# Building C with the gate in ScalarE's operand of the one-hot product while the top-k runs, one comparison on VectorE, and five paces set anew

## The chip, the cores and the metric

The kernel runs on one core of one Trainium2 chip. The metric is the device time of one execution in microseconds (us): three runs of the kernel before took 3491.34, 3493.19 and 3498.84 us, median 3493.19. Engines are named as in the profile: PE is TensorE, DVE is VectorE, ACT is ScalarE, POOL is GpSimd, SP is SyncE.

## The reference, cut to what matters

One encoder layer over 1024 tokens of width 1024: two attention branches, a merge, a layer norm, and then a layer of product-key experts. Only the last part is touched. Each token has 8 heads, each head picks 16 experts out of 128 x 128 by two top-16 searches over 128 keys and one over their sums:

```
s = jnp.einsum('thpd,hpkd->thpk', q, sub_keys)
top_s, top_i = lax.top_k(s, K)
cand_i = top_i[:, :, 0, :, None] * PEER_N_KEYS + top_i[:, :, 1, None, :]
...
gate = jax.nn.softmax(best_s, axis=-1)
h = jax.nn.gelu(jnp.einsum('thkd,td->thk', u_table[idx], xb))
return jnp.einsum('thk,thkd->td', gate * h, v_table[idx])
```

So each token has 128 selections: a key i, a key j and a gate. All of it is float32.

## The kernel before

The 1024 tokens are eight tiles of 128. Five of them (0, 1, 2, 6, 7) are **gathered**: for each of a token's 128 selections one row of `u` and one row of `v` (4 KB each) is fetched by an indirect DMA that POOL issues, 128 rows (512 KB) at a time. Three of them (3, 4, 5, `DENSE`) are **dense**: their hidden states are multiplied with all 16384 experts, and a table C of 128 x 128 gates per token says which count.

The end of the kernel, from `dense_block` on, is what matters here. It has two stages.

**Building C** (lines 1579 to 1627). Selection c of a token puts its gate at place (i, j). For one token this is a product of two one-hot matrices, A (128 selections x 128 keys i) and B (128 selections x 128 keys j), one of which carries the gate. `onehot(t4)` makes A (`a`) and B (`b`) for four tokens, 384 tokens in all, so 96 blocks. PE makes four matmuls of a block (tile `v`, "`v<-ab`"), and ACT copies the result out of PSUM in two parts, 44 columns into `C` (line 1623) and 84 into `S` (line 1624); each eight blocks SP writes `S` to DRAM (`cd`). Step k of the loop makes the operands of block k + 3 (`BLEAD`), the matmuls of block k, and the copies of block k - 1. The tile `ab` has four buffers, so the operands of block k + 4 wait for the matmuls of block k; `v` has three.

In `onehot`, `b` is made by DVE in four instructions, each a comparison with the key's number and a multiplication by the gate (line 1570). `a` is made by DVE in one comparison of 512 columns (line 1576) for even blocks. For odd blocks ACT makes it as Relu(1 - |n - i|): four Abs with the key's number as bias (line 1573) and one Relu of 512 columns (line 1574).

**The dense loop** (128 steps) multiplies hidden states with `u` (tile `b`, 24 matmuls a step) and the gated result with `v` (18 matmuls), and streams both tables, 1 MB a step, through SP's queue (`uraw<-ut`, `vraw<-vt`). ACT and DVE split the float32 data into two parts.

Two queues of other work are fed into both stages. `mm` calls `tick` for each matmul, which adds the matmul's nominal time times a rate to a credit, and steps are taken from the queue while the credit lasts. So the rates, not the time, set what stands beside what in the order of each engine.

- **V** (rate `RATEV`, first number in building C, second in the dense loop) handles the gathered tiles' `v` rows: a pair of gathers (line 1852, tile `vr`, or places lent by C), a copy of the gates into `win` by ACT (line 1879), and four matmuls (tile `pg`). 256 pairs in all. `win` has four slots, so a copy waits for the matmuls four pairs back.
- **B** (rate `RATEB`, first number in building C, second in the dense loop, third there once the last top-k is done) handles the top-k of tiles 4, 5 and 6 (`LATE`, tags k4, k5, k6), then the `u` rows of tile 6 (line 1469, and the dot product on DVE, line 1481) mixed with the top-k of tile 7, then tile 7's `u` and `v` rows. A dense tile's top-k must be complete before its blocks begin: `selections` forces it (k4 at block 32, k5 at block 64) and loads gate, i and j into `cT`.

PE's, DVE's and POOL's orders in this part are the order of the code. ACT's and SP's are set by the scheduler that builds the program.

Of the kernel before, what the change touches and what calls it, by code (L numbers as in the profile page):

```python
# [10 lines left out]
F32 = mybir.dt.float32  # L11
# [4 lines left out]
AF = mybir.ActivationFunctionType  # L16
OP = mybir.AluOpType
# [10 lines left out]
TKI = 1  # L28
RATEP = (0.975, 0.975, 0.87)

RATEB = (2.1, 0.562, 0.58)
RATEV = (4.2, 0.425)
SEL = (1, 2, 3)
DENSE = (3, 4, 5)
GATHERED = (0, 1, 2, 6)
# [1 line left out]
LATE = (4, 5, 6)  # L37
# [4 lines left out]
HALF, LOOP, GROUP, BLK = 44, 8, 4, 32  # L42
VCOST = 3.0
XAT = 14
AENG = "XY"
UPOOL = (0, 0)
VPAT = ()
VBUF = 3
# [226 lines left out]
def mm(g, o, l, r, start, stop_):  # L275
    g.pe.matmul(o, l, r, start=start, stop=stop_)  # L276
    n = 1
    for d in r.shape[1:]:
        n *= d
    us = max(n, 256) / 2400.0 if r.dtype == F32R else max(4 * n, 256) / 2400.0  # L280
    g.V.tick(us)
    if not g.V.busy:
        g.B.tick(us)
# [98 lines left out]
def run(gen):  # L382
    for _ in gen:
        pass
# [19 lines left out]
def body(ctx, g):  # L404
# [106 lines left out]
    g.pp = ctx.enter_context(tc.tile_pool(name="pp", bufs=1))  # L511
    C = g.pp.tile([128, len(DENSE), HALF, 128], F32, name="C")
    dense_block(g, C)


# [998 lines left out]
def dense_block(g, C):  # L1514
# [3 lines left out]
    dve, act, pool, sp, pe = g.dve, g.act, g.pool, g.sp, g.pe  # L1518
    tiles = DENSE
    nt = len(tiles)  # L1520
    n = nt * 128
# [13 lines left out]
    def hidden_states():  # L1535

        for i, t in enumerate(tiles):
            z = bp.tile([128, 2, 4, 128], F32, name="ab").rearrange("p a b c -> p (a b c)")
            sp.dma_start(z, g.x1d[t])
            for k in range(0, 8, 4):  # L1540
                yield
                pt = g.psV.tile([128, 4, 128], F32, name="v21")
                for u in range(4):
                    pe.transpose(pt[:, u, :], z[:, (k + u) * 128:(k + u + 1) * 128], ident)
                s = slice(i * 128, (i + 1) * 128)
                split(g, xh[:, k:k + 4, s], xl[:, k:k + 4, s], pt)

    def selections(i):

        if i == 0:  # L1550
            yield
            yield
        g.B.need(f"k{tiles[i]}")
        cij = bp.tile([128, 3, 128], F32, name="cij", bufs=1)
        sp.dma_start(cij, g.cijd[tiles[i]])
        yield
        pt = g.psV.tile([128, 4, 128], F32, name=f"v{i}1")
        for j in range(3):
            pe.transpose(pt[:, j, :], cij[:, j, :], ident)
        act.copy(cT[:, :, i * 128 - 128:i * 128], pt[:, 0:3, :])  # L1560
        yield

    def onehot(t4):

        cT_, t4_ = (g.rows.cT, t4) if t4 < 32 else (cT, t4 - 32)
        ab_ = bp.tile([128, 2, 4, 128], F32, name="ab")
        a, b = ab_[:, 0], ab_[:, 1]
        for u in range(4):
            t = slice(4 * t4_ + u, 4 * t4_ + u + 1)
            dve.tensor_scalar(b[:, u, :], g.iota, cT_[:, 2, t], cT_[:, 0, t], op0=OP.is_equal, op1=OP.mult)  # L1570
        if AENG[t4 % len(AENG)] == "Y":
            for u in range(4):
                act.activation(a[:, u, :], g.iota, AF.Abs, scale=-1.0, bias=cT_[:, 1, 4 * t4_ + u:4 * t4_ + u + 1])
            act.activation(a, a, AF.Relu, scale=-1.0, bias=1.0)
        else:
            dve.tensor_tensor(a, g.iota[:, None, :].to_broadcast([128, 4, 128]), cT_[:, 1, 4 * t4_:4 * t4_ + 4, None].to_broadcast([128, 4, 128]), op=OP.is_equal)
        return a, b

    g.B.rate, g.V.rate = RATEB[0], RATEV[0]
    zx = ExitStack()  # L1580
# [7 lines left out]
    with tc.tile_pool(name="bp", bufs=BLEAD + 1) as bp, tc.tile_pool(name="cj", bufs=2) as cj:  # L1588
        ab, pb = {}, {}
        cT = bp.tile([128, 3, n - 128], F32, name="cT", bufs=1)  # L1590
        for k in range(-BLEAD - 4, n4 + 1):
            e = k + BLEAD + 4
            if e % 32 in (0, 4) and e < n4:
                if e % 32 == 0:
                    sel = selections(e // 32)
                next(sel)
            if 0 <= k + BLEAD < n4:
                ab[k + BLEAD] = onehot(k + BLEAD)
            if k > 0 and (k + 8) % 32 == 0 and (k + 8) // 32 in later:
                g.rows.places.drop(later[(k + 8) // 32] + lent.get((k + 8) // 32, []))  # L1600
            if k > 0 and k % 32 == 0 and k // 32 in later:
                g.rows.leave(later[k // 32] + lent.get(k // 32, []))
                for p in lent.pop(k // 32, []):
                    g.keys.give(p)
            if 0 <= k < n4:
                a, b = ab.pop(k)
                pb[k] = g.psV.tile([128, 4, 128], F32, name=f"v{k % 3}0")
                for u in range(4):
                    mm(g, pb[k][:, u, :], a[:, u, :], b[:, u, :], True, True)
            if k == n4 - XAT:  # L1610
                xp = zx.enter_context(tc.tile_pool(name="xp", bufs=1, side="right"))
                xh = xp.tile([128, 8, n], F32R, name="xh")
                xl = xp.tile([128, 8, n], F32R, name="xl")
                xt = hidden_states()
            if xt and k % 2 == 0:
                next(xt, None)
            if k > 0:
                e = k - 1
                i, o = 4 * e // BLK, 4 * e % BLK
                if o == 0:  # L1620
                    S = cj.tile([128, 128 - HALF, BLK], F32, name="S")
                p = pb.pop(e).rearrange("p t j -> p j t")
                act.copy(C[:, e // 32, :, 4 * e % 128:4 * e % 128 + 4], p[:, 0:HALF, :])
                act.copy(S[:, :, o:o + 4], p[:, HALF:128, :])  # L1624
                if o + 4 == BLK:
                    sp.dma_start(g.cd[i], S)
        run(xt)
    g.B.rate, g.V.rate = RATEB[1], RATEV[1]
    u_hl, v_hl, c_hl, phs = {}, {}, {}, {}
# [99 lines left out]
    for j in range(128):  # L1729
# [14 lines left out]
        if f"k{LAST}" in g.B.done:  # L1744
            g.B.rate = RATEB[2]
        if j == 126:
# [3 lines left out]
        k = (j + 1 - LOOP) // 8 * nt  # L1750
# [279 lines left out]
```

## Time and profile before

| | |
|---|---|
| median of three runs | 3493.19 us |
| the profiled execution's own time | 3488.81 us |
| its span, first to last instruction | 3487.0 us |
| building C, first to last copy into `S` | 1763.7 to 2177.9 us |
| dense loop, first to last `h` | 2200.1 to 3450.9 us |
| DMA, mean over the span | 325 GB/s |
| granted TensorE clock, mean | 0.932 |

Instructions of one engine can overlap at their edges, so the duration of one is more than what it adds to a row of them; "busy" in a group or a window counts overlapped time once.

### The profile page before, as it was taken

How to read it: one execution, taken by the hardware profiler on the slowest of the kernel's cores; microseconds unless marked ns; L12 is line 12 of the kernel's file. 1: busy time of each engine (PE TensorE's matmuls, PEld its weight loads, DVE VectorE, ACT ScalarE, POOL GpSimd, SP SyncE). 2: the span in 40 equal slices, each digit the busy share in tenths (PEclk: the TensorE clock that was granted, in tenths of full speed). 3: DMA queues.
4: the chain of work that ended last, by engine and by line, in shares of the span. 5: the costliest groups of instructions: out<-in, count | busy, mean ns of one | idle time of the engine just before them, and what ended most of it. 6: DMA issues, size and time to landing. Idle time of an engine off the chain costs nothing.

```text
span 3487.0 us, 54632 instructions
## 1 busy us (share of the span) xinstructions
PE 3089.3 (89%) x20141; PEld 2301.4 (66%) x20141; DVE 2376.6 (68%) x5489; ACT 1140.0 (33%) x2380; POOL 1756.1 (50%) x1430
## 2 busy tenths in 40 slices
PE   7899898999998878789777777999999999999996
PEld 5577776885566666567633332688887777777875
DVE  3234523358988898987479865687777767677776
ACT  3443223232432222111134443334333333333332
POOL 2032115325565456553464567555756566566761
PEclk9999999998998887989988989999999999999998
DMA  8373347889989778989998899999999999999995
GB/s 282 118 250 113 98 151 264 296 320 324 306 301 368 255 271 309 352 323 373 369 377 340 340 371 392 376 371 372 409 409 406 400 401 391 402 400 397 399 398 196
DMA packets 366876, 1132.22 MB, mean 325 GB/s; under 512 B 49456, under 2 KB 85936, under 8 KB 364816
## 3 DMA queue, kind: packets, MB, share of 16 engines
q0 software_dynamic: 184448, 671.56, 50.8%
q1 hardware_dynamic: 165760, 428.06, 33.7%
q10 hardware_dynamic: 16400, 29.11, 2.2%
q8 instruction: 158, 2.59, 0.3%
q14 instruction: 110, 0.90, 0.1%
HBM read 995.94 MB, written 132.64 MB: 324 GB/s over the span
## 4 chain that ended last, share of the span: by engine, by line
PE 47%; DVE 19%; DMA 16%; issue 7%; POOL 3%; ACT 2%; another core or an unknown queue 0%; SPq 0%; ACTq 0%; POOLq 0%; DVEq 0%
PE b L276 12%; PE v L276 10%; DMA uraw<-ut 8%; PE pj L276 7%; PE s L276 5%; PE o L276 5%; DVE g L1481 4%; PE pg L276 3%; DMA g<-u,idx 3%; PE S L276 2%; DVE ab L1570 1%; POOL g L1469 1%; DMA vr<-v,ve 1%; PE a L276 1%; DMA wl<-whd 1%
## 5 line engine op out<-in xcount | busy, mean ns | idle before, releaser
L1469 POOL DMA_INDIRECT g<-u,idx x569 | 685.3, 1204 | 609.0 <-DVE hh L1481 311.8
L1481 DVE CUSTOM_DVE_ANT_0 g<-g,ext 128x1024 f32<-128x1024 f32 x569 | 701.1, 1238 | 85.2 <-DMA g<-u,idx 66.8
L1852 POOL DMA_INDIRECT vr<-v,ve x285 | 338.1, 1186 | 174.0 <-PE pg L276 74.5
L276 PE MATMUL b<-xh,uh 128*128 128x384 f32 x1024 | 354.3, 346 | 41.0 <-ACT h L1684 39.7
L294 POOL TENSOR_TENSOR wl<-wraw,wh 128x1024 fp32r<-128x1024 f32 x63 | 152.7, 2424 | 436.7 <-ACT wh L293 337.2
L276 PE MATMUL b<-xl,uh 128*128 128x384 f32 x1024 | 352.1, 344 | 0.0
L276 PE MATMUL b<-xh,ul 128*128 128x384 f32 x1024 | 351.7, 343 | 0.1
L294 DVE TENSOR_TENSOR ul<-uraw,uh 128x512 fp32r<-128x512 f32 x256 | 176.0, 690 | 223.1 <-ACT uh L293 205.0
L276 PE MATMUL v<-vl,ch 128*128 128x512 f32 x768 | 301.9, 393 | 0.7 <-DVE vl L294 0.6
L276 PE MATMUL v<-vh,ch 128*128 128x512 f32 x768 | 301.1, 392 | 0.1
L276 PE MATMUL v<-vh,cl 128*128 128x512 f32 x768 | 300.9, 392 | 0.0
L276 PE MATMUL pj<-xh,wh 128*128 128x512 f32 x624 | 283.7, 455 | 13.9 <-ACT xh L293 7.1
L293 ACT CAST uh<-uraw 128x512 fp32r<-128x512 f32 x256 | 157.2, 620 | 410.2 <-PE b L276 210.0
L276 PE MATMUL pg<-vr,win 128*32 128x512 f32 x1364 | 243.2, 641 | 46.8 <-DMA vr<-v,ve 38.7
L276 PE MATMUL pj<-xl,wh 128*128 128x512 f32 x624 | 257.8, 413 | 2.4 <-DVE xl L294 2.4
L276 PE MATMUL pj<-xh,wl 128*128 128x512 f32 x624 | 257.5, 413 | 0.0
L276 PEld LDWEIGHTS b<-xh,uh 128*128 128x128 f32 x1024 | 196.3, 192 | 62.2 <-ACT h L1684 48.1
L276 PEld LDWEIGHTS v<-ab 128*128 128x128 f32 x768 | 111.1, 214 | 187.8 <-issue 113.4
L293 ACT CAST vh<-vraw 128x512 fp32r<-128x512 f32 x256 | 156.1, 618 | 162.1 <-PE v L276 115.5
L276 PEld LDWEIGHTS b<-xl,uh 128*128 128x128 f32 x1024 | 196.1, 192 | 15.2 <-issue 10.9
L276 PEld LDWEIGHTS b<-xh,ul 128*128 128x128 f32 x1024 | 195.9, 191 | 11.5 <-issue 9.8
L276 PE MATMUL v<-ab 128*128 128x128 f32 x768 | 139.8, 320 | 71.2 <-ACT S L1624 20.6
(395 smaller groups left out, 6555.2 us busy)
## 6 DMA issues: line engine op xcount, KB each, us to landing
uraw<-ut SPq DMA_DIRECT2D x128, 512.0 KB
vraw<-vt SPq DMA_DIRECT2D x128, 512.0 KB
wraw<-w SPq DMA_DIRECT2D x72, 512.0 KB
wh<-whd SPq DMA_DIRECT2D x72, 512.0 KB
wl<-whd SPq DMA_DIRECT2D x72, 512.0 KB
whd<-wh SPq DMA_DIRECT2D x71, 512.0 KB
whd<-wl SPq DMA_DIRECT2D x71, 512.0 KB
cd<-S SPq DMA_DIRECT2D x12, 1344.0 KB
```

The lines of the kernel that those rows point to most:

```text
L276: g.pe.matmul(o, l, r, start=start, stop=stop_)
L293: g.act.copy(hi, src)
L294: (lo_eng or g.dve).tensor_sub(lo, src, hi.bitcast(F32))
L1469: pool.indirect_dma_start(out=place, out_offset=None, in_=A["uv"[n // 128]], in_offset=bass.IndirectOffsetOnAxis(ap=idx[:, n % 128:n % 128 ...
L1481: dve.tensor_tensor_reduce(out=gg, in0=gg, in1=xt, scale=1.0, scalar=0.0, op0=OP.mult, op1=OP.add, accum_out=hh[:, k:k + 1])
L1570: dve.tensor_scalar(b[:, u, :], g.iota, cT_[:, 2, t], cT_[:, 0, t], op0=OP.is_equal, op1=OP.mult)
L1852: g.pool.indirect_dma_start(out=place, out_offset=None, in_=g.A["v"], in_offset=bass.IndirectOffsetOnAxis(ap=self.meta[i][1][:, t:t + 1], ...
```

## The change

While k6 is not done, `onehot` takes another way: DVE makes `b` with one comparison of 512 columns and no gate, and ACT makes `a` with the gate in it, as Relu(gate - gate * |n - i|). This takes four Abs, as before, and four Relu of 128 columns each, with a scale (the gate's negative, from the new tile `cN`) and a bias (the gate), both one number a partition. All blocks made before k6 is done go this way, even and odd. Later blocks are made as before. `cN` is filled by one ACT instruction for each dense tile.

The paces: V's rate in building C goes from 4.2 to 4.6, in the dense loop from 0.425 to 0.399. B's rate in building C stays 2.1 until k4 is done and is 1.7 from there; in the dense loop it goes from 0.562 to 0.588, and after the last top-k from 0.58 to 0.598.

```diff
-RATEB = (2.1, 0.562, 0.58)
-RATEV = (4.2, 0.425)
+RATEB = (2.1, 0.588, 0.598)
+RATEV = (4.6, 0.399)
+RATEC = 1.7
...
-AENG = "XY"
...
         act.copy(cT[:, :, i * 128 - 128:i * 128], pt[:, 0:3, :])
+        act.mul(cN[:, i * 128:i * 128 + 128], pt[:, 0, :], -1.0)
...
         a, b = ab_[:, 0], ab_[:, 1]
+        if f"k{LATE[-1]}" not in g.B.done:
+            dve.tensor_tensor(b, g.iota[:, None, :].to_broadcast([128, 4, 128]), cT_[:, 2, 4 * t4_:4 * t4_ + 4, None].to_broadcast([128, 4, 128]), op=OP.is_equal)
+            for u in range(4):
+                t = slice(4 * t4_ + u, 4 * t4_ + u + 1)
+                act.activation(a[:, u, :], g.iota, AF.Abs, scale=-1.0, bias=cT_[:, 1, t])
+                act.activation(a[:, u, :], a[:, u, :], AF.Relu, scale=cN[:, 4 * t4 + u:4 * t4 + u + 1], bias=cT_[:, 0, t])
+            return a, b
...
-        if AENG[t4 % len(AENG)] == "Y":
+        if t4 % 2:
...
+        cN = bp.tile([128, n], F32, name="cN", bufs=1)
+        act.mul(cN[:, 0:128], g.rows.cT[:, 0, :], -1.0)
...
+            if f"k{LATE[0]}" in g.B.done:
+                g.B.rate = RATEC
```

Two places show how the instructions stand. On ACT, around the copies of blocks 33 and 34, before (`ab` holds both operands, `base` the numbers 0 to 127, `C`, `S` and `v` are as above):

```order
L1879 COPY win<-g_72 128x2
L1573 ACTIVATE ab<-base,cT 128x128 x4
L1623 COPY C<-v_15368 128x44x4
L1574 ACTIVATE ab<-ab 128x512
L1624 COPY S<-v_15368 128x84x4
L1879 COPY win<-g_72 128x2
L1623 COPY C<-v_15411 128x44x4
L1624 COPY S<-v_15411 128x84x4
L1879 COPY win<-g_72 128x2
```

And at the same copies in the changed kernel, whose later lines are numbered 12 higher:

```order
L1573 ACTIVATE ab<-base,cT 128x128 x2
L1574 ACTIVATE ab<-ab,cT,cN 128x128 x2
L1891 COPY win<-g_72 128x2
L1635 COPY C<-v_15451 128x44x4
L1636 COPY S<-v_15451 128x84x4
L1891 COPY win<-g_72 128x2 x4
L1573 ACTIVATE ab<-base,cT 128x128 x2
L1574 ACTIVATE ab<-ab,cT,cN 128x128 x2
L1573 ACTIVATE ab<-base,cT 128x128 x2
L1574 ACTIVATE ab<-ab,cT,cN 128x128 x2
L1635 COPY C<-v_15492 128x44x4
L1636 COPY S<-v_15492 128x84x4
```

Two Abs and two Relu alternate, each block has its eight, and the copies into `win`, which stood one or two to a block, now stand five together behind every fourth or third block.

On DVE, two blocks' operands among the instructions of k4's top-k (`s`, `ra`, `rank`), before:

```order
L1570 TENSOR_SCALAR ab<-base,g_72 128x128 x4
L1429 TENSOR_TENSOR s<-ra,rank 128x1024
L1430 TENSOR_TENSOR s<-s 128x1024
L1433 TENSOR_TENSOR s<-s 128x4x128
L1433 TENSOR_TENSOR s<-s 128x4x64
L1433 TENSOR_TENSOR s<-s 128x4x32
L1434 TENSOR_TENSOR ij<-s 128x64
L1570 TENSOR_SCALAR ab<-base,g_72 128x128 x4
L1576 TENSOR_TENSOR ab<-base,g_72 128x512
```

and in the changed kernel:

```order
L1570 TENSOR_TENSOR ab<-base,g_72 128x512
L1429 TENSOR_TENSOR s<-ra,rank 128x1024
L1430 TENSOR_TENSOR s<-s 128x1024
L1433 TENSOR_TENSOR s<-s 128x4x128
L1433 TENSOR_TENSOR s<-s 128x4x64
L1433 TENSOR_TENSOR s<-s 128x4x32
L1434 TENSOR_TENSOR ij<-s 128x64
L1570 TENSOR_TENSOR ab<-base,g_72 128x512
```

Four or five instructions a block have become one; the top-k's own stand as they stood.

Counted over the whole order, the two kernels' queues are at these points:

| at the end of building C | before | after |
|---|---|---|
| pairs of V multiplied, of 256 | 115 | 126 |
| `v` rows gathered (instructions of 128 rows) | 234 | 256 |
| `u` gathers of tile 6 | 31 | 18 |
| searches of the last top-k, of 16 | 12 | 6 |
| blocks made the new way, of 96 | 0 | 78 |

At step 76, where the changed kernel has just finished k6, it has gathered 18 `v` instructions more and 12 `u` instructions fewer than the kernel before had there (204 and 0 against 186 and 12). Between dense steps 0 and 30 it takes 29 pairs and 135 gathers where the kernel before takes 32 and 141, and from there to step 126 480 gathers against 483. Both finish both queues in the last steps of the loop.

## Prediction

> **What bounds the kernel now.** I read the windows first, cut where the stages change, then the copies into `S` as the clock of building C, then the waits. The windows:
>
> ```profile
> core 0: us, PE busy (x) PEld busy (x) DVE busy (x) ACT busy (x) POOL busy (x), PEclk, DMA share, GB/s
> 1764.00:2020.00 256.00, 190.15 (x1122) 90.21 (x1121) 228.17 (x1057) 116.02 (x381) 140.25 (x140) 0.85 0.91 343
> 2020.00:2078.00 58.00, 40.61 (x197) 16.63 (x197) 33.84 (x107) 22.36 (x78) 41.35 (x38) 0.85 1.01 393
> 2078.00:2178.00 100.00, 74.37 (x359) 29.04 (x358) 57.96 (x180) 33.67 (x110) 71.44 (x65) 0.93 1.01 392
> 2200.00:2480.00 280.00, 279.34 (x1492) 230.89 (x1493) 219.26 (x481) 109.75 (x219) 160.20 (x137) 0.99 0.99 375
> 2480.00:3414.00 934.00, 898.63 (x4737) 735.26 (x4736) 673.43 (x1022) 330.44 (x678) 579.84 (x481) 0.98 1.03 401
> ```
>
> From 1764 to 2020 us DVE is the busiest, 228.17 of 256 us, which is 89%; the DMA engines move 343 GB/s. From 2020 on DVE falls to under 60%, and the DMA moves 392 to 401 GB/s wherever PE does not run without a gap. In the dense loop PE is the limit until about 2480 (279.34 of 280 us), and after that the DMA: the chain of waits of that part has pieces like
>
> ```profile
> 2312.72 1.85 PE pg L276 x16
> ...
> 3265.27 19.90 DMA uraw<-ut
> ```
>
> The first piece is two pairs of V on PE in the first part of the loop, 0.93 us a pair; the second is a wait of 19.9 us for a table's transfer in the later part. So three limits follow each other: DVE for the first two thirds of building C, then the DMA, then PE for some 30 steps, then the DMA. How fast building C goes, the copies into `S` tell:
>
> ```profile
> L1624 ACT COPY S<-v x76: 417/442/487, 1763.7 to 2077.0; 128x336 f32<-128x336 f32 x76
> L1624 ACT COPY S<-v x96: 417/442/487, 1763.7 to 2177.9; 128x336 f32<-128x336 f32 x96
> ```
>
> 76 of them take 314 us, 4.1 us each, the last 20 about 100 us, 5 us each. The changed kernel uses its new way up to block 77, so I take building C apart at 2078 us.
>
> **The change, the first 76 steps.** What DVE loses and ACT gains is read from the tile `ab` between 1764 and 2078 us, and from single groups there:
>
> ```profile
> sum 314.00, PE 109.97 PEld 87.40 DVE 107.30 ACT 72.57; mean PE 54.99 PEld 43.70 DVE 53.65 ACT 36.28
> ...
> L1576 DVE TENSOR_TENSOR ab<-base,cT 128x512 f32<-128x512 f32 x24 | 16.4, 684 | 0.0
> L1573 ACT ACTIVATE ab<-base,cT 128x128 f32<-128x128 f32 x96 | 30.7, 393 | 10.4 <-remote 5.5 <-PE v L276 4.2 <-PE pg L276 0.6
> L1574 ACT ACTIVATE ab<-ab 128x512 f32<-128x512 f32 x38 | 24.0, 631 | 0.1
> ```
>
> DVE spends 107.3 us on operands there, and would spend 76 x 0.684 = 52 us, so 55 us go. Besides, it loses what the slower B pace puts later: most of the ten dot products of tile 6 that stand in this stretch (12.1 us), and four of the last top-k's searches. DVE then has at most 262 - 55 - 12 = 195 us of work in a stretch of 314 us, and is no longer the limit.
>
> ACT gains work. An Abs costs 0.295 us in a row of four, since the next may begin before it has ended:
>
> ```profile
> 1953.17 1.27 ACT L1573 ACTIVATE ab<-base,cT 128x128 f32<-128x128 f32 x4
> 1954.35 0.28 ACT L1623 COPY C<-v 128x176 f32<-128x176 f32 x1
> ```
>
> (1954.35 - 1953.17, over four). The new Relu with scale and bias from memory isn't in the trace at this size. Its nearest rows:
>
> ```profile
> L1129 ACT ACTIVATE kt<-kt,vec 128x512 f32<-128x512 f32 x8 | 6.3, 810 | 13.1 <-DVE kt L1127 13.1
> L1443 ACT ACTIVATE pf<-pf 128x128 f32<-128x128 f32 x3 | 0.9, 310 | 9.8 <-DVE pf L1442 9.8
> ```
>
> L1129 has both operands from memory and 512 columns, 0.18 us over L1574, which has none; on the 0.31 us of L1443 at 128 columns this makes 0.49. From below, it could be as cheap as an Abs, 0.295; from above, nothing overlaps, and it costs 0.49. I take 0.49 less the 0.1 us by which an Abs's 0.393 exceeds its pitch: 0.39, because the pairs of Abs and Relu in ACT's order leave each Relu's input finished one instruction earlier. A block then costs 4 x (0.295 + 0.39) = 2.74 us (2.36 to 3.14). ACT had 116.0 + 22.4 = 138.4 us of work in the stretch, 72.6 of it on `ab`. Now 73 blocks (the first five are made ahead of it) make 200 us, the ten or so further `win` copies 2 us, so 268 us (240 to 297).
>
> The Trainium skill, "ScalarE: Activation LUTs", section "What ACT_TABLE_LOAD costs", gives 186 ns and 0.833 ns a column, 93 ns for each operand from memory, and an overlap of 93 ns between neighbours. By it, as an estimate, a Relu has a pitch of 386 ns and the block costs 2.72 us; the sum would come out the same, and the trace agrees for Abs with 0.393 us.
>
> The DMA is the other limit. It moved 256 x 343 + 58 x 393, so 110.6 MB, in this stretch; 18 `v` instructions more and 12 `u` fewer, of 128 x 4 KB each, add 3 MB. At the 393 to 401 GB/s of the saturated windows 113.7 MB take 284 to 289 us.
>
> So ACT (268) and the DMA (287) are close, and neither will run without gaps: ACT waits in its order for PE, PE for ACT. DVE as the limit reached 89%. With that for ACT, 268 / 0.891 = 301 us, a little above the DMA's own. I take 301: **13 us less** than 314. The two bounds are 287 (the DMA alone, -27 us) and 297 / 0.891 = 333 (+19 us).
>
> **The last 20 steps.** Here the DMA was the limit (392 GB/s). The operands are as before for most blocks. The gathers rise from 67 to 70 instructions: 1.6 MB at 392 GB/s, **4 us more**.
>
> **The dense loop.** In the PE-bound part the changed kernel has three pairs fewer, 3 x 0.93 = **3 us less**. In the DMA-bound part it has three gathers fewer, 1.6 MB at 401 GB/s, **4 us less**. Six searches of the last top-k move to the first dozen steps, each five instructions like these and three short loads:
>
> ```profile
> L1374 DVE MAX8 tv<-tmp 128x8 f32<-128x128 f32 x52 | 15.3, 295 | 1.8
> ```
>
> That is at most 6 x 1.7 = 10 us on DVE, over 110 us in which DVE is 78% busy (219 of 280). I cost it at nothing, as it fits beside PE's unbroken work; if the matmuls' operands queue behind it on DVE, up to 4 us come back.
>
> **The VectorE rule that speaks against it.** The row above says 0.684 us for one comparison of 512 columns, and four of 128 columns with a multiplication cost 1.1 us:
>
> ```profile
> 1949.08 1.10 DVE L1570 TENSOR_SCALAR ab<-base,cT 128x128 f32<-128x128 f32 x4
> ```
>
> The Trainium skill, "VectorE: DVE Perf Modes", section "The perf-mode tier table (the rule you actually need)", has a float32 comparison with a scalar at twice the pace of one between tensors, so the single comparison should lose: by it, as an estimate, twice 1.1 us a block, 76 x 2.2 = 167 us, which would leave DVE at 310 of 314 us and the sum at -3. The trace does not agree: its one comparison takes 0.684 us, and the sum goes by that.
>
> **The sum.** -13 + 4 - 3 - 4 = -16 us, against the profiled execution's own 3488.8 us. The median of the runs, 3493.2, is 4.4 us above that execution; the runs compared are such runs, so the forecast is 3477 us.
>
> **The rivals.**
>
> - *The DMA alone is the limit.* ACT's gaps hide behind transfers: 287 us, -27 + 4 - 7 = -30, 3463 us. For it: the saturated windows hold 392 GB/s for 100 us on end. Against it: with k at 58 to 77 only two pairs are gathered ahead.
> - *Nothing is gained in building C.* ACT takes DVE's place at the same pace, 314 us, since the waits move with the bound: -3 us, 3490 us. The rows on ACT's waits in the same stretch speak for it:
>
> ```profile
> ACT win L1879 <- PE pg L276: 39.9, 20, 6.3
> ACT s L1427 <- DVE s L1430: 39.8, 9, 12.4
> ```
>
> ACT lost 40 us each to PE and to DVE in its order, which cost nothing while it had 175 us to spare. The second kind should go with a DVE that is ahead.
> - *ACT becomes a worse bound than DVE was* (slower). The place is the `win` copies, now five behind two or more blocks' eight instructions: PE's `pg` waits until ACT gets there, PE then stands some 3 us in each four steps (ACT 268 / 19 = 14 us, PE 110 / 19 for the blocks and 5.2 pairs of 0.93, 11 us), and places come free late, so that gathers start late. The stretch exceeds 314 us once a block costs over 2.9 us at 89%: (280 - 66 - 2) / 73. At the upper price of 3.14, 333 us: +19 + 4 - 7 = +16, 3509 us.
> - *The change doesn't take the new way.* Excluded by the order: 78 blocks have it.
>
> **How the numbers follow.** I give the forecast (3468 to 3485) 0.40, the DMA rival 0.17, no gain 0.20, the ACT rival 0.23. A measurement of this kernel can tell about 0.2%, 7 us, from no change. The first two are faster by more, 0.57; the third is within, 0.20; the fourth slower, 0.23. The range reaches from 3455, below the DMA rival, to 3508, just short of the ACT rival's own value.
>
> **What would show it.** In the changed kernel's windows of building C, ACT must be at about 85 to 90% and DVE at 60%; the 77th copy into `S` some 13 us earlier after the first than 313 us; a Relu at 0.49 us with a pitch of 0.39. If the DMA stays near 350 GB/s and PE's waits for `win` lead the list, the ACT rival is right; if the DMA is at 390 or more throughout, the first. The dense loop should be 5 to 8 us shorter. Wrong would be the forecast if a Relu costs more than 0.45 us of pitch, or if PE no longer runs unbroken in the first 30 dense steps, since then DVE's added top-k is in the way.

## The result, and the profile after

| | before | after |
|---|---|---|
| median, runs side by side | 3496.02 us (6 runs) | 3529.27 us (6 runs) |
| ratio, 95% interval | | 1.0087 [1.0063, 1.011] |
| the profiled execution's span | 3487.0 us | 3521.9 us |
| mean granted TensorE clock | 0.932 | 0.926 |

The kernel became slower by 0.87%, some 30 us (the medians differ by 33), outside the predicted range of 3455 to 3508. Cut at the same events, the two profiled executions differ by 34.9 us:

| stretch | forecast | before | after | difference |
|---|---|---|---|---|
| up to the first operand of building C | 0 | 1743.9 | 1747.3 | +3.4 |
| first operand to first copy into `S` | 0 | 19.8 | 23.0 | +3.2 |
| first to 77th copy into `S` | -13 | 314.5 | 347.6 | **+33.1** |
| 77th to 96th copy | +4 | 99.8 | 98.5 | -1.3 |
| to the first `h` | 0 | 22.2 | 17.6 | -4.6 |
| first to last `h` (dense loop) | -7 | 1250.8 | 1255.4 | +4.6 |
| behind the last `h` | 0 | 36.1 | 32.5 | -3.6 |

So nearly all of it lies where the change's new way is in use. The windows of the changed kernel, cut as those of before (the columns are busy time of each engine, granted clock, DMA share, DMA rate):

```profile
core 0: us, PE busy (x) PEld busy (x) DVE busy (x) ACT busy (x) POOL busy (x), PEclk, DMA share, GB/s
1770.00:2020.00 250.00, 172.23 (x1015) 78.40 (x1018) 142.77 (x641) 202.14 (x648) 135.94 (x136) 0.80 0.91 335
2020.00:2118.00 98.00, 69.99 (x387) 29.43 (x380) 47.17 (x198) 69.93 (x225) 49.94 (x52) 0.87 0.90 330
2118.00:2216.00 98.00, 73.48 (x360) 29.16 (x359) 50.86 (x152) 32.14 (x108) 67.77 (x64) 0.92 1.01 392
2234.00:2514.00 280.00, 278.99 (x1481) 231.10 (x1482) 226.56 (x531) 110.15 (x216) 161.55 (x135) 0.99 0.98 371
2514.00:3452.00 938.00, 890.99 (x4678) 736.16 (x4677) 680.92 (x1042) 328.88 (x668) 577.88 (x476) 0.97 1.02 395
```

DVE is relieved as forecast: 142.77 + 47.17 = 190 us, where the forecast had at most 195. ACT's 202.14 + 69.93 = 272 us is the forecast's 268. But ACT is only 78% busy (272 of 348), not 89%, and the DMA has fallen from 343 to 335 GB/s, and from 393 to 330 in the second window. No engine is full. The groups of `ab` on ACT show that its price wasn't the mistake (min/median/max of one in ns, then first and last start):

```profile
L1573 ACT ACTIVATE ab<-base,cT x184: 384/394/425, 1890.9 to 2093.5; 128x128 f32<-128x128 f32 x184
L1574 ACT ACTIVATE ab<-ab,cT,cN x184: 477/483/505, 1891.5 to 2094.2; 128x128 f32<-128x128 f32 x184
```

A Relu with both operands from memory takes 0.483 us (forecast 0.49), and two in a row 0.86 us (the rows of ACT below), a pitch of 0.38 (forecast 0.39). The waits from 1770 to 2118 us (us in total, times, longest) tell what is new:

```profile
PE pg L276 <- ACT win L1891: 79.2, 18, 8.0
DVE ab L1570 <- PE v L276: 67.7, 22, 6.2
ACT ab L1573 <- PE v L276: 20.1, 21, 2.6
ACT win L1891 <- PE pg L276: 19.3, 11, 8.0
```

PE waits 18 times, 4.4 us each, for a copy into `win` that stands on ACT behind whole blocks; before, PE's matmuls waited for none. ACT and DVE in turn wait for PE's `v`: DVE's `ab` 67.7 us where it was 19.3 us before (from 1764 to 2078 us). ACT's waits for `pg` are not new, they were 39.9 us before, but ACT then had time to spare. One period, PE's order first (start, us, instruction, idle time before it; a pair's four matmuls of the code are eight in the trace):

```profile
1930.66 1.94 PE L276 MATMUL pg<-vr,win 128*32 128x512 f32 x8 [5.71 <-ACT win L1891]
1932.52 1.65 PE L276 MATMUL v<-ab 128*128 128x128 f32 x6
...
1940.71 1.07 PE L276 MATMUL pg<-vr,win 128*32 128x512 f32 x8
1941.70 0.94 PE L276 MATMUL v<-ab 128*128 128x128 f32 x6
1950.65 1.08 PE L276 MATMUL pg<-vr,win 128*32 128x512 f32 x4 [8.01 <-ACT win L1891]
```

Then ACT's around the same copies:

```profile
1930.42 0.18 ACT L1891 COPY win<-g 128x2 f32<-128x2 f32 x1
...
1931.03 0.39 ACT L1891 COPY win<-g 128x2 f32<-128x2 f32 x3
1932.74 0.20 ACT L1891 COPY win<-g 128x2 f32<-128x2 f32 x1 [1.32 <-PE pg L276]
1934.21 0.69 ACT L1573 ACTIVATE ab<-base,cT 128x128 f32<-128x128 f32 x2 [1.27 <-PE v L276]
...
1936.17 0.86 ACT L1574 ACTIVATE ab<-ab,cT,cN 128x128 f32<-128x128 f32 x2
...
1943.51 0.69 ACT L1573 ACTIVATE ab<-base,cT 128x128 f32<-128x128 f32 x2 [1.89 <-PE v L276]
...
1950.40 0.20 ACT L1891 COPY win<-g 128x2 f32<-128x2 f32 x1
```

ACT puts five gates into `win` from 1930.42 to 1932.74 us and comes back at 1950.40. PE uses up what it got and stands from 1942.6 to 1950.65. When it starts again it is slow, and ACT waits for it. Windows of 4 us show the clock (columns as above):

```profile
1927.00:1931.00 4.00, 0.34 (x4) 0.20 (x8) 3.76 (x22) 4.00 (x14) 2.38 (x3) 0.74 1.01 387
1931.00:1935.00 4.00, 4.00 (x22) 1.56 (x14) 0.95 (x3) 1.41 (x8) 1.82 (x2) 0.50 0.73 235
1935.00:1939.00 4.00, 4.00 (x34) 2.02 (x30) 2.51 (x11) 3.27 (x11) 2.18 (x4) 0.90 0.82 275
1939.00:1943.00 4.00, 3.64 (x28) 1.65 (x21) 1.83 (x9) 2.62 (x8) 3.08 (x4) 1.00 0.92 306
1943.00:1947.00 4.00, 0.00 (x0) 0.00 (x0) 3.32 (x7) 3.49 (x11) 2.11 (x3) 0.88 0.88 310
```

After 5.7 us without work PE runs at 0.50, and eight `pg` matmuls take 1.94 us in place of 1.07. In those 4 us ACT is busy for 1.41 us. The DMA falls to 235 GB/s: `pg` ends late, so the places for gathers come free late (POOL's waits for `pg` ahead of gathers into `vr` and `C` are 53.0 us from 1770 to 2118 us, and were 38.3 before). (The Trainium skill, "TensorE: Matmul & The Clock Gate", section "HAM oscillation — how this bites in real kernels", has a gap in PE's work of over some 3.4 us put the clock to half. By that rule these gaps of 5.7 and 8.0 us should do it, and the trace agrees with its 0.50.) How much of the 33 us is the clock's was not separated by a run; the run with early copies below bounds a part of it.

### The profile page after: what moved, and what is told of

Its sections match the earlier page's. It is cut to its first block, busy times and chain, and to the rows that moved or that the text cites. A ratio compares the mean times of both kernels' runs of the same rounds, so it can differ in the third digit from the quotient of the medians.

```text
span 3521.9 us, 54938 instructions
## 1 busy us (share of the span) xinstructions
PE 3093.6 (88%) x20141; PEld 2305.8 (65%) x20141; DVE 2318.4 (66%) x5216; ACT 1283.4 (36%) x2814; POOL 1751.5 (50%) x1430
## 4 chain that ended last, share of the span: by engine, by line
PE 53%; DVE 14%; DMA 13%; issue 6%; ACT 6%; POOL 2%; another core or an unknown queue 1%; ACTq 0%; SPq 0%; POOLq 0%; DVEq 0%
PE b L276 13%; PE v L276 13%; PE pj L276 7%; DMA uraw<-ut 5%; PE pg L276 5%; PE s L276 5%; PE o L276 5%; DVE g L1481 4%; DMA g<-u,idx 3%; ACT ab L1574 2%; PE S L276 2%; ACT ab L1573 2%; POOL g L1469 2%; DMA vr<-v,ve 1%
## 5 line engine op out<-in xcount | busy, mean ns | idle before, releaser
L1864 POOL DMA_INDIRECT vr<-v,ve x285 | 325.4, 1142 | 175.6 <-issue 59.0
L276 PE MATMUL pg<-vr,win 128*32 128x512 f32 x1364 | 255.4, 658 | 107.2 <-ACT win L1891 55.9
L276 PE MATMUL v<-vh,ch 128*128 128x512 f32 x768 | 301.1, 392 | 0.6 <-ACT ch L293 0.6
L294 DVE TENSOR_TENSOR vl<-vraw,vh 128x512 fp32r<-128x512 f32 x256 | 175.0, 689 | 26.0 <-ACT vh L293 19.2
```

What stands on the lines that cost most here:

```text
L294: (lo_eng or g.dve).tensor_sub(lo, src, hi.bitcast(F32))
L1864: g.pool.indirect_dma_start(out=place, out_offset=None, in_=g.A["v"], in_offset=bass.IndirectOffsetOnAxis(ap=self.meta[i][1][:, t:t + 1], ...
```

## The experiments

Ratios are against runs of the kernel before on the same chip, taken in the same set of runs. "76 steps" is the time from the first to the 77th copy into `S` in the profiled execution: 314.5 us before, 347.6 after. The time ahead of building C, where the work is the same, alone ranges from 1734 to 1765 us between the profiled executions of the first twelve runs, so a profile's whole span says less than its stages.

### The paces, and the operands, each alone

The first run puts the paces alone into the kernel before:

```diff
-RATEB = (2.1, 0.562, 0.58)
-RATEV = (4.2, 0.425)
+RATEB = (2.1, 0.588, 0.598)
+RATEV = (4.6, 0.399)
+RATEC = 1.7
...
+            if f"k{LATE[0]}" in g.B.done:
+                g.B.rate = RATEC
```

> The kernel before with the five new paces alone; operands as before. Theory L (PE waits at the row matmuls for copies into win that stand late in ScalarE's order, since the blocks' eight instructions are ahead of them) and theory W (ScalarE's work itself is the bound): the paces are not the cause, so within 10 us of the kernel before, the 77 copies into S within 325 us. Theory P (the paces are the cause: more row matmuls and gathers in building C, more of B in the dense loop): 20 to 35 us slower than before.

Measured: 3488.45 us, ratio 0.9985 [0.9966, 1.0004], 76 steps in 311.9 us. The paces by themselves do no harm to the old operands.

The second takes the same lines out of the changed kernel:

> The changed kernel with the old paces; the new operands alone. k6 is then done some ten steps earlier, so about 68 blocks go the new way. L and W: building C still slow, the first 76 copies 335 to 350 us, the whole 20 to 35 us slower than before. P: within 10 us of the kernel before.

Measured: 3516.26 us, ratio 1.0067 [1.0028, 1.0106], 76 steps in 324.3 us, less than the 335 to 350 expected; only 68 blocks go the new way (k6 is done earlier). PE waits 64.9 us for `win` from 1770 to 2100 us. The operands alone make the kernel slower.

### The copies into win given to DVE

```diff
-            g.act.copy(win[:, :, o:o + 1], c4[:, :, m:m + 1])
+            (g.act.copy if f"k{LATE[-1]}" in g.B.done else g.dve.tensor_copy)(win[:, :, o:o + 1], c4[:, :, m:m + 1])
```

> The changed kernel with VectorE instead of ScalarE making the copies into win while the new way is taken. ScalarE's eight instructions a block stay. L: PE's 80 us of waits for win on ScalarE go, the first 76 copies into S take 290 to 315 us, the whole is 25 to 45 us faster than the changed kernel. W: ScalarE is left with 5 us less work, so the first 76 copies take 335 to 345 us and the whole gains at most 10 us.

Measured: 3512.98 us, ratio 1.0061 [1.0038, 1.0084]: 0.26% better than the change, less than the 25 to 45 us expected, and the two intervals overlap. The waits of PE and of the blocks in the profiled execution (its slowest one, 347.2 us for the 76 steps):

```profile
DVE ab L1570 <- PE v L276: 68.0, 44, 4.5
...
PE pg L276 <- DVE win L1891: 57.3, 41, 4.4
ACT ab L1573 <- PE v L276: 37.2, 30, 3.5
```

The wait moved with the copy. On DVE it stands behind the block's comparison, which waits for `v`, as on ACT it stands behind the block's Abs. So it isn't ACT's load that makes PE wait, but that the copy is queued behind something that waits for PE.

### ACT's order in building C as the code is written

```diff
-    mans(g, ALL)
+    mans(g, ALL | {mybir.EngineType.Activation})
...
+            if e == 80:
+                mans(g, ALL)
```

The scheduler no longer sets ACT's order up to step k = 73 (`e` is k + 7). One or two `win` copies then stand behind each block's eight instructions, instead of five behind every third or fourth.

> The changed kernel with ScalarE in the order of the code while the new way is taken: one or two copies into win behind each block's eight instructions, not five behind every third or fourth. If the bunches are what costs (L, bunches), the first 76 copies take 300 to 325 us. If any place behind a block's eight instructions costs (L, every block), PE waits once a step, and they take 345 us or more. W: 335 to 350 us, as the work is the same.

Measured: 3652.88 us, ratio 1.0473 [1.0437, 1.0509], 471 us for the 76 steps:

```profile
DVE ab L1570 <- PE v L276: 197.6, 66, 6.4
...
PE pg L276 <- ACT win L1893: 174.2, 71, 5.1
...
ACT ab L1573 <- PE v L276: 127.9, 64, 3.0
```

Now PE waits once in every block, 71 times: the gates wait for the operands of a block, those for the matmuls of an earlier block, and those stand on PE behind `pg`, which waits for the gates. The scheduler's groups of five had softened this loop.

### The copies into win two pairs ahead

```diff
-            g.act.copy(win[:, :, o:o + 1], c4[:, :, m:m + 1])
+            for k_ in range(k, k + 2 * 2 * (not self.pairs) + 1, 2):
+                if k_ > self.ahead and k_ // 128 == i:
...
+                    g.act.copy(win[:, :, o_:o_ + 1], c_[:, :, m_:m_ + 1])
+                    self.ahead = k_
```

In building C each gate is copied two pairs before its own; `win` has four slots, so there is room. Nothing is left out or added.

> The changed kernel with the copy into win made two pairs ahead of its matmuls in building C, still on ScalarE; the scheduler then places one or two behind each block instead of five behind every third or fourth. Theory L2 (late copies make PE idle for some 6 us in each bunch, the granted clock falls to a half meanwhile, PE's first matmuls then run slowly, and ScalarE waits for them): PE's waits for win fall from 80 us below 25, the clock in building C rises from 0.80 to 0.85 or more, the first 76 copies into S take 295 to 320 us and the whole is 25 to 45 us faster than the changed kernel. Theory W (the work on ScalarE): at most 10 us faster.

Measured: 3500.91 us, ratio 1.0022 [1.0004, 1.004], 76 steps in 321.6 us, just above the 295 to 320 expected; the profiled execution is its fastest. PE's waits for `win` have come down from 79.2 us to 4.4. The 76 steps of the changed kernel, then those of this run, and of this run the part from the first to the 58th copy into `S`:

```profile
1770.40:2118.00 347.60, 242.06 (x1397) 107.83 (x1398) 189.57 (x837) 271.67 (x871) 185.49 (x187) 0.82 0.91 334
...
1758.30:2079.90 321.60, 238.83 (x1396) 105.18 (x1396) 188.95 (x833) 269.76 (x870) 185.18 (x187) 0.90 0.95 360
1758.30:1987.60 229.30, 168.75 (x1052) 77.07 (x1052) 147.30 (x661) 205.99 (x665) 136.78 (x137) 0.91 0.97 371
```

In the first 57 steps the clock is 0.91 and the DMA at 371 GB/s; ACT is 90% busy (205.99 of 229.30), the share that the forecast had given it. Over all 76 steps it is 84% (269.76 of 321.60). So, by the ratios of two sets, some 0.65% of the change's 0.87% was the place of these copies; by the profiled executions, 26.0 of the 33.1 us. The engines do nearly the same work in both, and PE's busy time differs by 3.2 us at a clock of 0.82 and 0.90: on PE itself, slow matmuls are a small part of the 26 us. What ACT and DVE lost in waiting for them is not separated.

The same with the early copies on DVE:

> As the run before this one, but with the early copies made by VectorE while the new way is taken. L2: as that one or up to 10 us faster, since ScalarE is rid of them; VectorE's copies no longer stand between a block's comparison and its pair's matmuls, so PE's wait for win on VectorE, 67 us when they were not early, falls below 20. W: as the changed kernel.

Measured: 3499.32 us, 1.0014 [0.9992, 1.0035], 320.9 us. Which engine copies makes no difference that these runs can tell once the copies are early.

The early copies and the new paces with the old operands:

> The old operands, the new paces and the early copies into win. L2: the old way had no bunches, since ScalarE had time, so it is within 7 us of the paces alone (ratio 0.9985). If early copies are a gain of their own, without the new operands, it is 10 us or more faster than those.

Measured: 3485.38 us, 0.9975 [0.9959, 0.9991], 311.1 us (in its fastest execution): 15.5 us faster than the same with the new operands, in the same set of runs. So even without the waits the new operands cost time. The same with the new way on odd blocks only:

> The changed kernel with early copies, but the new way on odd blocks alone; even blocks go as before, wholly on VectorE. ScalarE's work falls by some 90 us against the changed kernel, VectorE's rises by some 30. L2: 5 to 15 us faster than the kernel with early copies and all blocks the new way. W: 25 us or more faster than that one, as ScalarE is the bound there.

Measured: 3489.91 us, 0.9985 [0.9968, 1.0003], 11 us faster than with all blocks the new way, as L2 expected; its profile (321.3 us) is of its slowest execution. And the early copies alone, in the kernel before:

> The kernel before, old operands and old paces, with nothing changed but that ACT's copies into win are put two pairs ahead in building C. Theory L (the place of the win copies costs time only where ACT's order is crowded with blocks of eight instructions): before has no wait of PE for win to speak of, so the time stays within 5 us of before (ratio 0.9985 to 1.0015), and the 0.25% that the early copies with the new paces gained is the paces' part. Theory E (the early copies are worth something by themselves): 7 to 10 us faster than before, ratio about 0.9975.

Measured: 3492.75 us, 1.0004 [0.9985, 1.0024], 313.4 us. They are worth nothing where ACT's order isn't crowded.

### Was DVE the limit at all?

Three runs take work from one engine and give it to none. Two leave the product with the gate out of `b` while k6 is not done (one comparison of 512 columns, `a` as before; "light `b`" from here on); the third leaves the gate out of the new way's Relu (one Relu of 512 columns, with early copies):

```diff
-        for u in range(4):
+        early = f"k{LATE[-1]}" not in g.B.done
+        if early:
+            dve.tensor_tensor(b, g.iota[:, None, :].to_broadcast([128, 4, 128]), cT_[:, 2, 4 * t4_:4 * t4_ + 4, None].to_broadcast([128, 4, 128]), op=OP.is_equal)
+        for u in range(0 if early else 4):
...
-                act.activation(a[:, u, :], a[:, u, :], AF.Relu, scale=cN[:, 4 * t4 + u:4 * t4 + u + 1], bias=cT_[:, 0, t])
+            act.activation(a, a, AF.Relu, scale=-1.0, bias=1.0)
```

DVE lighter in the kernel before:

> The kernel before (old operands, old paces, late win copies) with b made by one comparison without the gate while k6 is not done; the product with the gate is left out there. DVE falls from 0.9 to about 0.8 of the first two thirds, ACT has no more to do. Theory D: 314 us fall by the 32 us that DVE loses, or to the bytes' own 287 us at about 0.95, 295 to 302 us; ratio 0.995 to 0.997. Theory M: what paces the 76 steps is when V and B hand out their work and when transfers come, not DVE; 310 to 316 us, ratio 0.9985 to 1.0015.

Measured: 3470.49 us, 0.993 [0.9911, 0.995], 76 steps in 294.6 us, the DMA at 380 and 372 GB/s there. DVE was the limit, as the prediction had it, and relieving it at no cost to ACT gives 20 us in the 76 steps (25 us by the medians), more than theory D expected. It doesn't give all of the 32 us that DVE loses; the DMA share there is 0.98, which fits with transfers as the next limit.

DVE lighter with the new paces and early copies:

> Old operands, new paces, early win copies (the fastest kernel so far, 311 us from the first to the 77th copy into S, DVE 0.91 and 0.82 busy in the first two thirds), with b made by one comparison of 512 columns without the gate while k6 is not done; the product with the gate is left out there. DVE loses 76 x (1.10 - 0.68) = 32 us, ACT gains nothing. Theory D (DVE is the limit of the first two thirds of building C, as the prediction had it): the 76 steps fall by 10 us or more, to 301 us or less, and the time is 10 us or more below that kernel's, ratio about 0.994 or less. Theory M (DVE at 90% is not the bound; transfers are, which already move 390 to 396 GB/s there): the 76 steps stay within 5 us of 311, ratio 0.996 to 0.999.

Measured: 3487.06 us, 0.9975 [0.9957, 0.9992], the same ratio as with the heavy DVE; 76 steps in 319.0 us in the profiled execution, its slowest. Here the relief gave nothing. The heavy form had this from its first to its 58th copy:

```profile
1761.30:1984.30 223.00, 185.25 (x1061) 81.42 (x1060) 192.22 (x880) 105.83 (x352) 140.12 (x139) 0.91 1.01 393
```

The DMA share was already 1.01 there.

ACT lighter in the changed kernel with early copies:

> The changed kernel with early win copies (about 0.2% slower than before; ACT 0.92 and 0.88 busy in the first two thirds, 322 us for the 76 steps), with the four Relu of a block replaced by one of 512 columns without scale and bias from memory; the gate is left out there. A block costs ACT 4 x 0.295 + 0.63 = 1.8 us in place of 2.74, so ACT loses 70 us of the stretch, and DVE stays at 0.61. Theory A (with the wait for win gone, ACT is the bound that DVE was): the 76 steps fall from 322 to 311 us or less, the time to 3485 us or less, ratio 0.9975 or less. Theory M (nothing on the engines bounds it, the transfers do): within 5 us of 322, ratio 1.000 to 1.003.

Measured: 3490.5 us, 0.9991 [0.9974, 1.0009], 316.3 us, between the two expectations: ACT's load is worth about 0.3% (1.0022 with the full load, in another set; the two intervals just touch), and something else holds the rest. In its first 57 steps ACT is busy for only 150.60 of 225.60 us, and the DMA share is 1.00.

### The paces again, with DVE relieved

Two of those runs contradict each other unless the paces or the early copies eat the relief. In the next runs the kernel before itself takes 3452 to 3456 us, some 40 us less than above, so ratios are compared, and medians only inside a set. Light `b`, new paces, late copies:

> The kernel before with b made by one comparison without the gate while k6 is not done (the product with the gate is left out there), the new paces and late win copies. With the old paces this gave a ratio of 0.993 and 295 us for the 76 steps. Theory R (the new paces eat the relief: they put some 7 MB more into a stretch that is at the transfers' limit, 7 MB at 390 GB/s being 18 us, and the dense loop gives nothing back): ratio 0.996 to 0.999, 76 steps at 305 to 320 us. Theory Q (the early copies ate it): ratio 0.991 to 0.994, 76 steps at 297 us or less.

Measured: 3454.25 us, 1.0002 [0.9989, 1.0016], 304.5 us. It isn't the early copies. The change's own operands with the old paces and early copies:

> The change's operands with the old paces and early win copies. With late copies this gave 1.0067, with the new paces and early copies 1.0022. Theory R: without the new paces the relief of DVE can show; ACT at 92% is then the bound (68 blocks of 2.74 us and its other 66 us make some 255 us, at 0.89 to 0.92 280 to 290 us for the same share of the 76 steps, the eight old blocks behind them included some 295 to 305), ratio 0.994 to 0.999. Theory Q, or a theory by which ACT's extra work itself costs the time through the waits of PE and DVE behind it: ratio 1.000 to 1.004.

Measured: 3452.22 us, 1.0003 [0.9987, 1.0019], theory Q's ratio, though the 76 steps take 288.3 us, less than theory R's 295 to 305. From the first to the 58th copy:

```profile
1747.60:1953.50 205.90, 152.19 (x999) 73.81 (x1002) 158.88 (x760) 204.05 (x658) 125.95 (x128) 0.93 1.00 391
```

ACT is busy for 204.05 of 205.90 us, and the DMA share is 1.00, so both are at their limit. PE again waits for `win`, 23.8 us in the 76 steps. The 76 steps are short, but the first copy comes 13.8 us after the first operands, since the first five blocks' operands (2.7 us each) all stand ahead of it on ACT. With the new way on odd blocks alone it is 6.3 us:

> The same with the new way on odd blocks alone (even ones as before): DVE loses 34 x 0.42 = 14 us, ACT gains 34 x 0.94 = 32 us and stays at some 60%. Theory R: about half of the 24 us that the full relief gained, ratio 0.995 to 0.998, and below the odd form with the new paces (0.9985). Theory Q: 0.9985 or more, as with the new paces.

Measured: 3441.46 us, **0.9968 [0.9955, 0.9981]**, 76 steps in 294.9 us. This is the best version with nothing left out: faster than the kernel before and, by the ratios, than the changed one (the same with B's new paces was not tried). Where its 10.8 us over the run with all blocks come from is not shown: from the first operand to the 77th copy the two profiled executions take 301.1 and 302.1 us, and 8.6 of the 10.0 us between their spans lie ahead of building C, where the work is the same. The last three runs share one set and take V's and B's paces apart, with light `b` and late copies. V's new paces only:

> The kernel before with b made by one comparison without the gate while k6 is not done (the product with the gate is left out there), late win copies, V's new paces (4.6, 0.399) and B's old ones. Theory R (more bytes in a stretch at the transfers' limit, with nothing back in the dense loop): V's pace brings the bytes into building C, so this is the bad half: 10 us or more above the same with old paces, ratio 0.997 or more if that stands at 0.993. Theory Q (the paces are not the cause, the two chips differ): within 5 us of the same with old paces.

B's new paces only:

> The same with V's old paces (4.2, 0.425) and B's new ones (2.1, 1.7 once k4 is done, then 0.588 and 0.598). B's pace takes transfers and DVE work out of building C. Theory R: no slower than with old paces in building C; with the added work in the dense loop, within 7 us of the old paces, ratio 0.991 to 0.996. Theory B (B's pace is the bad half, as k6 is then done ten blocks later and the last top-k's searches stand in the dense loop): 10 us or more above the old paces.

All paces old:

> The kernel before with b made by one comparison without the gate while k6 is not done (the product with the gate is left out there), all paces old: the run that gave 0.993, on the chip of the other two. Theory R: 0.992 to 0.995 again. Theory Q (what the relief is worth hangs on the chip): 0.997 or more on a chip with the faster kernel before.

Measured: 1.0034 [1.0022, 1.0047] (3467.62 us), 0.9958 [0.9943, 0.9972] (3437.16 us) and 0.9975 [0.9962, 0.9988] (3447.36 us). V's paces cost 20 us, B's gain 10. V's cost is what theory R expected; B's gain is more than its 7 us. The third run is outside what theory R expected for it, and where theory Q had it; but this run and the one of 0.993 were on a chip of the same number, so the chip alone is not the reason. The windows of the 76 steps and the dense loop, with V's paces:

```profile
1746.40:2067.20 320.80, 274.42 (x1422) 108.28 (x1414) 236.44 (x973) 145.85 (x469) 209.44 (x206) 0.93 1.01 395
2191.80:3433.90 1242.10, 1203.57 (x6351) 994.24 (x6352) 919.94 (x1538) 453.76 (x911) 739.63 (x603) 0.99 1.00 383
```

with B's:

```profile
1737.40:2018.20 280.80, 243.14 (x1351) 104.63 (x1344) 214.81 (x895) 141.26 (x459) 175.40 (x176) 0.94 1.01 395
2132.90:3396.00 1263.10, 1219.19 (x6424) 998.24 (x6425) 938.17 (x1610) 453.06 (x921) 764.09 (x633) 0.98 1.01 392
```

and with the old ones:

```profile
1747.40:2039.20 291.80, 246.44 (x1350) 105.74 (x1342) 235.43 (x971) 140.56 (x458) 191.07 (x187) 0.93 1.01 398
2161.50:3416.30 1254.80, 1219.27 (x6424) 1000.73 (x6425) 918.01 (x1533) 454.98 (x919) 743.48 (x620) 0.98 1.01 389
```

The DMA share is 1.01 in all three: the steps take as long as their bytes (320.8 x 395 = 126.7 MB, 110.9 MB, 116.1 MB). V's paces put 10.6 MB more there for 29 us, and the dense loop returns 12.7 us; B's take 5.2 MB out for 11 us and cost 8.3 us later. What comes back is less than half in the one case and three quarters in the other.

The full relief by light `b` gave 0.993 in one set and 0.9975 in this; why it is worth less where the kernel before is faster stays open, since that kernel wasn't profiled in the faster sets. This light kernel itself was profiled in both. Its two executions differ by 25.0 us, of which 10.2 lie ahead of building C, 10.9 between the first operand and the first copy, and 2.8 in the 76 steps (294.6 and 291.8 us).

## Why the prediction was wrong, point by point

- *DVE is the limit of the first two thirds of building C*: right. Taking about 0.42 us a block from it, and nothing else, shortened the 76 steps from 314.5 to 294.6 us.
- *The cost of the operands* on both engines: right to a few per cent. DVE's `ab` work fell from 107.3 to 52.6 us (forecast 52). The estimate of 2.2 us a block for the single comparison, which the prediction set aside for its 0.684 us, doubled the time of four instructions, where one instruction takes their place.
- *ACT at 89% like DVE, so 301 us*: **this step failed**, in two ways. First, the 89% is DVE's share of the 256 us to 2020 us, but the 268 us of work that it was put to are those of all 76 steps, and over these DVE was busy for 262 of 314 us, 83%. With 83% the same rule gives 321 us, 7 us more than before instead of 13 less. With the copies early, ACT did reach 90% in the first 57 steps, which took 229.3 us where they had taken 227.8 before, and 84% over all 76, which took 321.6 us; that is near this sum, but one kernel that agrees does not prove the rule. Second, the forecast carried a share of busy time from one engine to another. DVE's long list of top-k instructions needs nothing from PE; ACT's eight instructions a block wait for `v`, and the gates that PE needs stand behind them. In the changed kernel ACT stood at 78%, and the 76 steps took 26.0 us more than with the copies early.
- *The ACT rival* named the place (five `win` copies behind blocks, gathers late), but priced it at 3 us in each four steps and 333 us in all. PE waited 4.4 us, 18 times, and the steps took 347.6 us. The price held PE's and ACT's work side by side, and left out that each then also waits for the other (ACT 20.1 us for `v`, 19.3 for `pg`), after each gap at half the clock; how much of the difference each of these makes was not tried. The order printed ahead of the prediction showed the five copies, so this rival could have been given more than its 0.23.
- *The start of building C* had no term. Five blocks' operands (5 x 2.74 = 13.7 us) stand ahead of the first copy on ACT, and gaps among them (last section) make 8.3 us: 23.0 us where the kernel before took 19.8, +3.2 us.
- *The last 20 steps*, +4: -1.3. The rate is 392 GB/s before and after, and the bytes did not rise (99.8 x 392 = 39.1 MB, 98.5 x 392 = 38.6 MB).
- *The dense loop*, -7: +4.6. Its first 30 steps, which PE bounds, took 280.8 us where they had taken 281.6 (forecast -3). In the later part the bytes left but the rate fell with them, 401 to 395 GB/s. The paces alone gave 1251.3 us for the loop, the same as before, so "bytes less times a saturated rate" didn't hold over the loop as a whole. Where the other 4 us come from was not tried; the two executions of the kernel with light `b` and old paces differ by 3.5 us in this loop (1251.3 and 1254.8), so they may be no more than the spread.
- *No gain in building C* as the waits move: what was left when the copies were early (1.0022) is nearest to this rival, with ACT at 84% of the 76 steps in place of DVE's 83%.
- *The DMA alone* (287 us): seen once DVE is light (280.8 to 291.8 us at a DMA share of 1.01, with V's old paces), not in the changed kernel. There the paces were counted as 3 MB more, and hidden; the 76 steps moved 116 MB (347.6 x 334) where they had moved 111.

## What to carry to other kernels

Before work is moved to an idle engine, look for what small things that engine hands to others, and for what the moved work itself waits for: a small copy queued behind an instruction that waits for its own consumer makes a loop, and no share of busy time shows it. Hand such copies out ahead first, then try moving less than all: half the blocks gave 0.9968 here, all of them 1.0003, though the profiles don't show where that difference lies. When a share of busy time is taken as a limit, take it over the same stretch as the work. Paces tuned for one limit must be set again for the next: all five together did no harm while DVE was the limit (0.9985), and V's cost 20 us when the transfers were.

## What the hardware showed that was not expected

At the start of building C some Relus of the changed kernel started late in a row that nothing on ACT interrupts; later in the stage no gap ahead of a Relu is longer than 0.23 us:

```profile
1756.13 0.68 ACT L1573 ACTIVATE ab<-base,g 128x128 f32<-128x128 f32 x2
1758.55 0.49 ACT L1574 ACTIVATE ab<-ab,g,cN 128x128 f32<-128x128 f32 x1 [1.74 <-remote]
1759.25 0.49 ACT L1574 ACTIVATE ab<-ab,g,cN 128x128 f32<-128x128 f32 x1 [0.21 <-ACT ab L1574]
1759.65 0.68 ACT L1573 ACTIVATE ab<-base,g 128x128 f32<-128x128 f32 x2
1762.79 0.49 ACT L1574 ACTIVATE ab<-ab,g,cN 128x128 f32<-128x128 f32 x1 [2.46 <-remote]
```

Gaps of 1.74 and 2.46 us stand ahead of instructions whose input ACT itself had just made. Eight such gaps, from 1753 to 1768 us, sum to 8.3 us. Like gaps stand in the profiles of the operands with the old paces, of the late copies on DVE and of both runs with early copies and all blocks the new way and the new paces. None longer than 0.25 us stands in the run with ACT's order as the code is written, in those with odd blocks alone, nor in the run with all blocks the new way, old paces and early copies, which was in a faster set: there the same instructions ran at their pitch of 0.38 us (five blocks in 13.6 us). The DMA was full in both cases (a share of 1.03, 409 GB/s from 1753 to 1768 us here and 411 GB/s from 1734 to 1748 there), so a full DMA alone does not make them. What held the Relus is not in the trace.
